# A gated FFN on Trainium2: up-projection as a 2x2 block product with seven products, down-projection as a stage of its own

## The chip, the core and the metric

The kernel runs on one core of a Trainium2 chip. TensorE (PE in the profile) multiplies, VectorE (DVE), ScalarE (ACT) and GpSimd (POOL) do the element work, and the sync engine's queue (SP) issues most transfers. The metric is the device time of one execution in microseconds (us), the median of several executions.

## The reference, cut to what matters

Two transformer blocks run one after the other on 1024 tokens of width 1024. Only the end of the second block is touched. There the reference is:

```
mix = sigmoid(ga) * (oa @ w_branch_a) + sigmoid(gb) * (ob @ w_branch_b)
x = x + mix @ w_out
h = rmsnorm(x, norm_ffn_w)
u = causal_dwconv(h @ w_up, conv_ffn_w) + conv_ffn_b      # 3 taps along the tokens
gate, up = split(u, 2, axis=-1)                           # 2816 features each
x = x + (silu(gate) * up) @ w_down
return rmsnorm(x, norm_final_w)
```

## The kernel before

All products run in fp32r with split operands. `split` takes an fp32 value to hi (an ACT cast, L59) and lo (a DVE subtraction of hi from the value, L62), and `acc3` or `gemm_fm` multiply hi by hi, hi by lo and lo by hi. So one product of a 128-row block costs three matmuls, all recorded at L41. Transposes are matmuls with the identity, recorded at L44.

The order within each engine's queue comes from a scheduler, which moves instructions of neighbouring steps past each other; each engine then runs its own queue strictly in order.

The end of the second block has these stages:

- `phase2_branch` makes the mix, feature-major, as hi and lo tiles of 8 x 128 features by 1024 tokens.
- `phase2_wout` loads x from DRAM (L1700), scales it (L1705), and adds mix @ w_out in blocks of 128 tokens by 256 columns (L1735). As the token tiles t finish, `post(t)` does the norm (ACT L1714, a chain of small DVE operations, DVE L1716), eight transposes and two splits into h hi and lo. The two halves (gate, up) of the first up-projection, `ff0`, then start.
- `phase2_ffn` runs 11 groups of two feature blocks j. For each j, gate and up are two products of 128 features by 1024 tokens, with 8 blocks of 128 inputs, 3 split products and 2 token halves: 96 matmuls of 512 columns per j, into the two-bank PSUM tiles `big`. The conv reads PSUM: an ACT identity with the first tap and the bias (L1763), and two DVE taps (L1767). Silu (ACT, L1789), the gate-up product (DVE, L1795) and its split into `ah` and `al` follow. After two j, `ah` and `al` go through the down-projection at once: 16 PSUM blocks with 6 matmuls each, and each block is added into `xs` by DVE (L1808).
- In the last group the sums of squares (L1814) and `phase2_final` (L1821 to L1831) follow each token tile: a chain of small operations, and the scaling (L1830, or ACT L1824 and POOL L1825 for t of 0 and 2), and a transfer out.

Weights come in 512 KB pieces through SP's queue, are split on ACT and DVE, and have two raw buffers (`wuraw`) and one (`wdraw`).

Of the kernel before, what the change touches and what calls it, by code (L numbers as in the profile page):

```python
# [6 lines left out]
F32 = mybir.dt.float32  # L7
F32R = mybir.dt.float32r
# [3 lines left out]
ALU = mybir.AluOpType  # L12
# [21 lines left out]
class Build:  # L34
# [1633 lines left out]
    def phase2_branch(self):  # L1668
        nc, tc, I = self.nc, self.tc, self.I
        mh = self.mp.tile([128, 8, 1024], F32R, name="mixh")  # L1670
        ml = self.mp.tile([128, 8, 1024], F32R, name="mixl")
        self.mix = (mh, ml)
        b2 = self.b2
        for sl in range(4):
            wab = self.w_b0 if sl == 0 else [
                self.load_w(b2, I[nm][sl], 256, ks=4, kb=2, tag="wa", rawbufs=2, bufs=6) for nm in ("w_ba", "w_bb")]
            for mm in range(2):
                m = sl * 2 + mm
                sg = [self.sg0[m]] if sl == 0 else []
                for a in range(len(sg), 2):  # L1680
                    t = b2.tile([128, 1024], F32, name="sg", bufs=4)
                    nc.sync.dma_start(t, self.sgd[a * 8 + m])
                    sg.append(t)
# [7 lines left out]
                self.split(mh[:, m], ml[:, m], sg[0])  # L1691

    def phase2_wout(self):
        nc, tc, I = self.nc, self.tc, self.I
        xs = self.xs = self.xp.tile([128, 8, 1024], F32, name="xs")
        hi = self.hp.tile([128, 8, 1024], F32R, name="hhi")
        lo = self.hp.tile([128, 8, 1024], F32R, name="hlo")
        self.h = (hi, lo)
        for t in range(8):
            nc.sync.dma_start(xs[:, t], self.xacc[t * 128:(t + 1) * 128, :])  # L1700
        wo = self.b2
        nf = wo.tile([128, 1024], F32, name="sg", bufs=4)
        self.load_row(nf, I["norm_final"])
        for t in range(8):
            nc.vector.scalar_tensor_tensor(xs[:, t], xs[:, t], self.r1[:, t:t + 1], nf, op0=ALU.mult, op1=ALU.mult)  # L1705

        nm = wo.tile([128, 1024], F32, name="sg", bufs=4)
        self.load_row(nm, I["norm_ffn2"])
        XN = [wo.tile([128, 1024], F32, name="sg", bufs=4) for _ in range(2)]

        def post(t):
            ss = self.sm.tile([128, 8], F32, name="ssx")[:, :1]
            xn = XN[t % 2]
            nc.scalar.activation(xn, xs[:, t], AF.Square, accum_out=ss)  # L1714
            rs = self.rsqrt(ss, 1.0 / 1024)
            nc.vector.scalar_tensor_tensor(xn, xs[:, t], rs, nm, op0=ALU.mult, op1=ALU.mult)  # L1716
            s = slice(t * 128, (t + 1) * 128)
            for f in range(0, 8, 4):
                ps = self.pa(2, 4)
                for i in range(4):  # L1720
                    self.tp(ps[:, i * 128:(i + 1) * 128], xn[:, (f + i) * 128:(f + i + 1) * 128])
                self.split(hi[:, f:f + 4, s], lo[:, f:f + 4, s], ps.rearrange("p (a b) -> p a b", a=4))
# [3 lines left out]
        for hf in range(2):  # L1726
            for n in range(4):
                W = load(I["w_out2"][n])
                for t in range(hf * 4, hf * 4 + 4):
                    ps = self.pa(0, 2)  # L1730
                    s = slice(t * 128, (t + 1) * 128)
                    for k in range(8):
                        self.acc3(ps[:, :256], (self.mix[0][:, k, s], self.mix[1][:, k, s]), W[k], k, k == 7)
                    cs = slice(n * 256, (n + 1) * 256)
                    nc.vector.tensor_add(xs[:, t, cs], xs[:, t, cs], ps[:, :256])  # L1735
# [5 lines left out]
        w = load(I["w_up2"][0])  # L1741
        self.ff0 = []
        for a in range(2):
            ps = self.big()
            self.gemm_fm(ps, w, a * 128, self.h, half_outer=True)
            self.ff0.append(ps)

    def phase2_ffn(self):
        nc, tc, I = self.nc, self.tc, self.I
        xs = self.xs  # L1750
        G = 2
        with self.pool("ff") as fp:
            nf = fp.tile([128, 1024], F32, name="nf")
            self.load_row(nf, I["norm_final2"])

            def up(j):
                return self.load_w(fp, I["w_up2"][j], 256, ks=8, kb=4, tag="wu", rawbufs=2, bufs=3)

            def conv(ps, m, parts=1):
                t = fp.tile([128, 1024], F32, name="cacc", bufs=3)  # L1760
                w = 1024 // parts
                for c in range(0, 1024, w):
                    nc.scalar.activation(t[:, c:c + w], ps[:, c:c + w], AF.Identity,  # L1763
                                         scale=self.col("conv_f", 88 + m), bias=self.col("conv_fb", m))
                    for tap in range(1, 3):
                        b = max(c, tap)
                        nc.vector.scalar_tensor_tensor(t[:, b:c + w], ps[:, b - tap:c + w - tap],  # L1767
                                                       self.col("conv_f", (2 - tap) * 44 + m), t[:, b:c + w],
                                                       op0=ALU.mult, op1=ALU.add)
                return t  # L1770

            for grp in range(11):
                A = []
                for jj in range(G):
                    j = grp * G + jj
                    if j > 1:
                        w = up(j)
                    if j:
                        acc = []
                        for a in range(2):  # L1780
                            ps = self.big()
                            end = j == 21 and a
                            self.gemm_fm(ps, w, a * 128, self.h, half_outer=end)
                            acc.append(conv(ps, j + 22 * a, 2 if end else 1))
# [219 lines left out]
```

## Time and profile before

| | us |
|---|---|
| median of 3 runs | 2929.35 (2927.75 to 2936.22) |
| the profiled execution, its own time | 2934.21 |
| its span | 2932.4 |
| PE busy | 2726.3 (93%) |
| DVE busy | 1765.5 (60%) |
| ACT busy | 1133.0 (39%) |
| POOL busy | 722.2 (25%) |

The span runs from the first to the last instruction on the chip; the execution's own time is 1.8 us longer. Shares of busy time are means over some ten stages with different limits, so the stage in question has to be read by itself: it is the last quarter of the span, from about 2150 us on. In the profile's slices POOL is at zero there up to the last 25 us.

### The profile page before, as it was taken

To read this page: it belongs to the slowest core of one execution; us is meant where nothing else is said; L and a number is where in the kernel's file an instruction comes from. 1 tells how busy PE (TensorE), PEld (TensorE's weight loads), DVE (VectorE), ACT (ScalarE), POOL (GpSimd) and SP (SyncE) were. 2 spreads that over 40 slices of the span, in tenths; PEclk is the share of its full clock that TensorE was granted. 3 is DMA by queue.
4 is the path that set the end of the run, shared out by engine and by line. 5 is a ranking of instruction groups with operands and counts; after the bars stand their busy time and mean duration, and the time that the engine had idled before them with its cause. 6 is when DMAs were issued, how large, how long until landed. Compare 5 with 4: busy or idle time off the path is not lost. (4 is left out here: it accounts for less than half of the span.)

```text
span 2932.4 us, 36530 instructions
## 1 busy us (share of the span) xinstructions
PE 2726.3 (93%) x14132; PEld 2183.9 (74%) x14132; DVE 1765.5 (60%) x2641; ACT 1133.0 (39%) x1762; POOL 722.2 (25%) x686
## 2 busy tenths in 40 slices
PE   6999998889948999699999899999999999999997
PEld 3886675555737777588889788778898888888886
DVE  3655568786687998756436333576565554455545
ACT  4445554444225666543321223463143222222223
POOL 1004425444344877412121332220000000000000
PEclk8999999999968999899999999999999999999999
DMA  6113300000567999512453544303432111111111
GB/s 223 41 57 112 106 37 1 1 22 33 172 221 255 373 373 362 171 42 88 158 182 116 185 150 141 100 23 110 164 100 67 51 57 44 50 51 43 44 36 58
DMA packets 180845, 338.75 MB, mean 116 GB/s; under 512 B 17672, under 2 KB 105736, under 8 KB 178368
## 3 DMA queue, kind: packets, MB, share of 16 engines
q1 hardware_dynamic: 162272, 270.13, 27.6%
q0 software_dynamic: 18400, 66.28, 7.1%
q8 instruction: 111, 1.82, 0.3%
q14 instruction: 62, 0.51, 0.1%
HBM read 282.88 MB, written 53.49 MB: 115 GB/s over the span
## 5 line engine op out<-in xcount | busy, mean ns | idle before, releaser
L62 DVE TENSOR_TENSOR mlo<-mraw,mhi 128x2048 fp32r<-128x2048 f32 x63 | 225.0, 3597 | 10.6 <-ACT mhi L59 10.6
L41 PE MATMUL big<-hhi,whi 128*128 128x512 f32 x656 | 210.6, 400 | 0.0
L41 PE MATMUL big<-hhi,wuhi 128*128 128x512 f32 x672 | 209.8, 389 | 0.0
L41 PE MATMUL big<-hlo,whi 128*128 128x512 f32 x656 | 208.6, 396 | 0.0
L41 PE MATMUL big<-hhi,wulo 128*128 128x512 f32 x672 | 208.2, 389 | 0.0
L41 PE MATMUL big<-hlo,wuhi 128*128 128x512 f32 x672 | 208.2, 389 | 0.0
L41 PE MATMUL big<-hhi,wlo 128*128 128x512 f32 x656 | 207.5, 395 | 0.0
L59 ACT CAST mhi<-mraw 128x2048 fp32r<-128x2048 f32 x96 | 181.7, 1912 | 55.4 <-PE big L41 29.3
L62 POOL TENSOR_TENSOR mlo<-mraw,mhi 128x2048 fp32r<-128x2048 f32 x33 | 165.5, 5022 | 74.9 <-ACT mhi L59 74.1
L1825 POOL TENSOR_TENSOR wuraw<-wuraw,nf 128x1024 f32<-128x1024 f32 x2 | 5.8, 2898 | 718.8 <-ACT rst L100 714.8
L1808 DVE TENSOR_TENSOR xs<-xs,t 128x512 f32<-128x512 f32 x176 | 117.9, 685 | 83.3 <-PE t L41 83.2
L1767 DVE SCALAR_TENSOR_TENSOR cacc<-big,cols,cacc 128x1023 f32<-128x1023 f32 (+2 forms) x90 | 113.1, 1257 | 76.6 <-ACT cacc L1763 74.9
L62 DVE TENSOR_TENSOR wlo<-wraw,whi 128x512 fp32r<-128x512 f32 (+5 forms) x124 | 80.6, 660 | 124.9 <-ACT whi L59 124.4
L41 PEld LDWEIGHTS big<-hhi,wuhi 128*128 128x128 f32 x672 | 126.2, 188 | 26.2
L41 PEld LDWEIGHTS big<-hhi,wulo 128*128 128x128 f32 x672 | 126.1, 188 | 26.2
L41 PEld LDWEIGHTS big<-hlo,wuhi 128*128 128x128 f32 x672 | 126.1, 188 | 26.2
L805 ACT ACTIVATE P<-t 128x512 f32<-128x512 f32 x160 | 95.1, 598 | 129.4 <-PE t L41 127.2
L41 PEld LDWEIGHTS big<-hlo,whi 128*128 128x128 f32 x656 | 122.9, 189 | 26.3
L41 PEld LDWEIGHTS big<-hhi,wlo 128*128 128x128 f32 x656 | 122.8, 189 | 26.0
L41 PE MATMUL t<-wdhi,ah 128*128 128x512 f32 x352 | 137.8, 391 | 1.4 <-ACT ah L59 1.2
L41 PEld LDWEIGHTS big<-hhi,whi 128*128 128x128 f32 x656 | 121.0, 189 | 23.6
L41 PE MATMUL t<-wdlo,ah 128*128 128x512 f32 x352 | 137.2, 390 | 0.0
(607 smaller groups left out, 6939.0 us busy)
## 6 DMA issues: line engine op xcount, KB each, us to landing
mraw<-in_w_gate SPq DMA_DIRECT2D x32, 1024.0 KB, 12.9
mraw<-in_w_up SPq DMA_DIRECT2D x32, 1024.0 KB, 13.3
mraw<-in_w_down SPq DMA_DIRECT2D x32, 1024.0 KB, 9.9
wmod<-in_w_mod SPq DMA_DIRECT2D x48, 512.0 KB, 5.9
wuraw<-in_w_up SPq DMA_DIRECT2D x42, 512.0 KB, 3.5
wraw<-in_w2a SPq DMA_DIRECT2D x72, 256.0 KB, 2.8
wdraw<-in_w_down SPq DMA_DIRECT2D x22, 512.0 KB, 3.2
gxd<-gx POOLq DMA_DIRECT2D x8, 1024.0 KB, 5.0
```

The lines of the kernel that those rows point to most:

```text
L41: self.nc.tensor.matmul(out, lhsT, rhs, start=start, stop=stop)
L59: nc.scalar.copy(hi, src)
L62: (nc.vector if lo_eng == "dve" else nc.gpsimd).tensor_sub(lo, src, hi.bitcast(F32))
L805: nc.scalar.activation(P, ps, AF.Exp, scale=self.sc_mla)
L1767: nc.vector.scalar_tensor_tensor(t[:, b:c + w], ps[:, b - tap:c + w - tap], self.col("conv_f", (2 - tap) * 44 + m), t[:, b:c + w], op0=ALU ...
L1808: nc.vector.tensor_add(xs[:, t, cs], xs[:, t, cs], ps)
L1825: nc.gpsimd.tensor_mul(y, y, nf)
```

## The change

**What it does.** The inputs of the up-projection (1024 features) are cut in two halves of 512, and so are the tokens. For one j the weights are four blocks (gate and up, by two feature halves) and h is four blocks (two feature halves by two token halves). Instead of eight block products, Winograd's form of Strassen's scheme takes seven, P1 to P7, each with 4 k-blocks and 3 split products: 12 matmuls of 512 columns, 84 per j. The sums that it needs are:

- of h, once: B11, B21, t1, t2 (in pool `hp3`, made in `post` and `put`) and t3, t4, B22 (made by `late` in buffers of the mix);
- of the weights, per j: S0, S1, S2, S4, four POOL operations of 128x512 on SBUF (L1834, L1835, L1852, L1857);
- of the products, per j: five DVE additions of a PSUM bank and an SBUF tile (L1844, L1851, L1855, L1861, L1865), two ACT copies out of PSUM (L1841, L1847), and two POOL additions on SBUF (L1859, L1864).

All seven weight operands per j are split after the sums (7 ACT casts, 7 DVE subtractions of 128x512). The products now land in four single-bank PSUM tiles in rotation, the sums go to four SBUF buffers for gate and up in turns, and the conv reads those (ACT L1824, DVE L1826). The gate-up product runs on POOL (L1868), and POOL's queue sends it to DRAM as `zd[j]` (L1869). x goes to DRAM too (`xsd`).

After the 22 j, the down-projection runs for each half of the tokens: 11 pairs of j, each with z reloaded and split, w_down reloaded and split, and 48 matmuls into eight PSUM banks that collect over all 22 j. So the number of its matmuls stays at 1056, and the DVE additions into `xs` fall from 176 to 16. w_down is loaded and split twice. `phase2_final` now runs for four token tiles at each half's end. The number of 128x128 transposes after w_out rises from 64 to 112.

```diff
     def phase2_wout(self):
...
+        def post(t):
+            normed(t)
+            x = XN[t]
+            if t < 4:
+                put("11", t, x[:, :512])
+                put("21", t, x[:, 512:])
+                return
+            y = XN[t - 4]
+            t2 = b3.tile([128, 512], F32, name="t2", bufs=2)
+            nc.vector.tensor_sub(y[:, :512], x[:, :512], y[:, :512])
+            nc.vector.tensor_sub(t2, x[:, 512:], y[:, :512])
+            put("t1", t - 4, y[:, :512])
+            put("t2", t - 4, t2)
+            nc.gpsimd.tensor_sub(x[:, :512], x[:, 512:], x[:, :512])
+            nc.gpsimd.tensor_sub(y[:, 512:], y[:, 512:], t2)
...
+        late("t3", "mh1", [XN[4 + i][:, :512] for i in range(4)])
+        late("t4", "ml1", [XN[i][:, 512:] for i in range(4)])
+        late("22", "mh0", [XN[4 + i][:, 512:] for i in range(4)])
...
     def phase2_ffn(self):
...
-            for grp in range(11):
...
-                        ah = fp.tile([128, 1024], F32R, name="ah", bufs=2 * G)
...
-                        nc.vector.tensor_add(xs[:, t, cs], xs[:, t, cs], ps)
...
+            for j in range(22):
+                raw = raw_of(I["w_up2"][j].rearrange("p (b n) -> p b n", b=4))
+                S = [fp.tile([128, 512], F32, name="S", bufs=3) for _ in range(3)]
+                nc.gpsimd.tensor_add(S[0], raw[:, 2], raw[:, 3])
+                nc.gpsimd.tensor_sub(S[1], S[0], raw[:, 0])
+                if j > 1:
+                    p1 = self.prod(self.pa(), op(raw[:, 0]), B["11"])
+                else:
+                    p1, p2 = self.ff0[j]
+                s = self.fa.tile([128, 512], F32, name="s", bufs=2)
+                nc.scalar.copy(s, p1)
+                p6 = self.prod(self.pa(), op(S[1]), B["t2"])
+                u2 = half(0)
+                nc.vector.tensor_add(u2, p6, s)
+                p5 = self.prod(self.pa(), op(S[0]), B["t1"])
+                c5 = half(1)
+                nc.scalar.copy(c5, p5)
+                if j > 1:
+                    p2 = self.prod(self.pa(), op(raw[:, 1]), B["21"])
+                g, u = gu(), gu()
+                nc.vector.tensor_add(g[:, :512], p2, s)
+                nc.gpsimd.tensor_sub(S[2], raw[:, 0], raw[:, 2])
+                p7 = self.prod(self.pa(), op(S[2]), B["t3"])
+                u3 = half(2)
+                nc.vector.tensor_add(u3, p7, u2)
+                S4 = fp.tile([128, 512], F32, name="S", bufs=3)
+                nc.gpsimd.tensor_sub(S4, raw[:, 1], S[1])
+                u4 = half(3)
+                nc.gpsimd.tensor_add(u4, u2, c5)
+                p3 = self.prod(self.pa(), op(S4), B["22"])
+                nc.vector.tensor_add(g[:, 512:], p3, u4)
+                tg = conv(g, j)
+                p4 = self.prod(self.pa(), op(raw[:, 3]), B["t4"])
+                nc.gpsimd.tensor_add(u[:, 512:], u3, c5)
+                nc.vector.tensor_add(u[:, :512], p4, u3)
+                tu = conv(u, j + 22)
+                nc.scalar.activation(tg, tg, AF.Silu)
+                nc.gpsimd.tensor_mul(tg, tg, tu)
+                nc.gpsimd.dma_start(self.zd[j], tg)
...
+                for bt in range(2):
...
+                    for kp in range(11):
+                        z = gu()
+                        for kk in range(2):
+                            nc.sync.dma_start(z[:, kk * 512:(kk + 1) * 512],
+                                              self.zd[kp * 2 + kk, :, bt * 512:(bt + 1) * 512])
...
-        if t in (0, 2):
+        if t in (4, 6):
```

**The loop.** DVE's queue before, over the end of one group and the next two j (`wuraw`, `wdraw` are raw weights, hi and lo their split, `cacc` the conv):

```order
L62 TENSOR_TENSOR wdlo<-wdraw,wdhi 128x1024 x2
L1767 SCALAR_TENSOR_TENSOR cacc<-big,cols,cacc 128x1023
L1767 SCALAR_TENSOR_TENSOR cacc<-big,cols,cacc 128x1022
L62 TENSOR_TENSOR wulo<-wuraw,wuhi 128x1024 x2
L1767 SCALAR_TENSOR_TENSOR cacc<-big,cols,cacc 128x1023
L1767 SCALAR_TENSOR_TENSOR cacc<-big,cols,cacc 128x1022
L1795 TENSOR_TENSOR cacc<-cacc 128x1024
L62 TENSOR_TENSOR al<-cacc,ah 128x1024
```

and DVE's queue now, in the middle of the loop, with the number of each buffer (`Ah` and `Al` are a split operand, `raw` raw weights, `ml0` the SBUF buffers of the sums, `t0` to `t3` PSUM banks, `s` the copy of P1):

```order
L62 TENSOR_TENSOR Al_19966<-raw_19957,Ah_19965 128x512
L1826 SCALAR_TENSOR_TENSOR cacc_19800<-ml0_18520,cols_73,cacc_19800 128x1023
L1826 SCALAR_TENSOR_TENSOR cacc_19800<-ml0_18520,cols_73,cacc_19800 128x1022
L62 TENSOR_TENSOR Al_19985<-S_19960,Ah_19984 128x512
L1844 TENSOR_TENSOR ml0_18520<-t1_19833,s_19831 128x512
L62 TENSOR_TENSOR Al_20003<-S_19959,Ah_20002 128x512
L62 TENSOR_TENSOR Al_20021<-raw_19957,Ah_20020 128x512
L1851 TENSOR_TENSOR ml0_18520<-t3_19869,s_19831 128x512
L62 TENSOR_TENSOR Al_20040<-S_19961,Ah_20039 128x512
L1855 TENSOR_TENSOR ml0_18520<-t0_19888,ml0_18520 128x512
```

POOL's queue before, from w_out to the end (three rows of norm weights, then the two products of `phase2_final`):

```order
L829 DMA sg_17036<-in_norm_final 128x1024
L829 DMA sg_17046<-in_norm_ffn2 128x1024
L829 DMA nf_18409<-in_norm_final2 128x1024
L1825 TENSOR_TENSOR wuraw_22459<-wuraw_22459,nf_18409 128x1024
L1825 TENSOR_TENSOR wuraw_22526<-wuraw_22526,nf_18409 128x1024
```

and POOL's queue now, one j of the loop, eight rows that come 22 times:

```order
L1835 TENSOR_TENSOR S_19960<-S_19959,raw_19957 128x512
L1864 TENSOR_TENSOR ml0_18520<-ml0_18520 128x512
L1852 TENSOR_TENSOR S_19961<-raw_19957 128x512
L1868 TENSOR_TENSOR cacc_19777<-cacc_19777,cacc_19800 128x1024
L1869 DMA zd_18516<-cacc_19777 128x1024
L1857 TENSOR_TENSOR S_20056<-raw_19957,S_19960 128x512
L1834 TENSOR_TENSOR S_20109<-raw_20107 128x512
L1859 TENSOR_TENSOR ml0_18520<-ml0_18520 128x512
```

The taps moved from PSUM to SBUF operands, the additions into `xs` and the gate-up product left DVE, the splits of weight sums stand between the additions of the j before, and POOL has work in the loop.

**The start of the FFN.** PE's queue before, at the last transposes (`sg` is the normed tile, `big` the first up-projection):

```order
L44 MATMUL t_18216<-ident,sg 128x128 x4
L44 MATMUL t_18223<-ident,sg 128x128 x4
L41 MATMUL big<-hhi,walo 128x512
L41 MATMUL big<-hhi,wahi 128x512
L41 MATMUL big<-hlo,wahi 128x512
L41 MATMUL big<-hhi,walo 128x512
```

and now (t3 and t4 are put out of buffers of `mh` and `ml`, `B21` is an operand of P2, `Bt2` of P6):

```order
L41 MATMUL big<-B21l,wahi 128x512
L41 MATMUL big<-B21h,walo 128x512
L44 MATMUL t_18427<-ident,ml_17603 128x128 x4
L44 MATMUL t_18434<-ident,ml_17603 128x128 x4
L44 MATMUL t_18441<-ident,ml_17603 128x128 x4
L44 MATMUL t_18448<-ident,ml_17603 128x128 x4
L44 MATMUL t_18456<-ident,mh_17602 128x128 x4
L44 MATMUL t_18463<-ident,mh_17602 128x128 x4
L44 MATMUL t_18470<-ident,mh_17602 128x128 x4
L44 MATMUL t_18477<-ident,mh_17602 128x128 x4
L41 MATMUL t_18534<-Bt2h,Ah 128x512
L41 MATMUL t_18534<-Bt2l,Ah 128x512
```

Eight groups of four transposes now stand in a row, with no product between them, ahead of the loop's first matmul.

**From up to down.** SP's queue now, at the end of the loop, with the engines and queues that a row waits for in brackets (before, w_down's loads stand between those of w_up, and nothing is reloaded):

```order
L1809 DMA raw_21779<-in_w_down2 128x2x1024 [waits DMAHW3_49,DVE_49,Pool_49]
L1809 DMA raw_21855<-in_w_down2 128x2x1024 [waits DMAHW4_49,DVE_49,Pool_49]
L1881 DMA xt_21769<-xsd_17069 128x1024 [waits DMASW0_49,PE_49]
L1881 DMA xt_21771<-xsd_17069 128x1024 [waits DMASW1_49]
L1881 DMA xt_21773<-xsd_17069 128x1024
L1881 DMA xt_21775<-xsd_17069 128x1024
L1881 DMA xt_22699<-xsd_17069 128x1024
L1881 DMA xt_22701<-xsd_17069 128x1024
L1881 DMA xt_22703<-xsd_17069 128x1024 [waits DMAHW5_49]
L1885 DMA ml0_18520<-zd_18516 128x512 [waits DMASW0_49,DMAHW6_49,DVE_49,Activation_49]
L1885 DMA ml0_18520<-zd_18516 128x512 [waits DMAHW7_49,DMASW1_49]
L1881 DMA xt_22705<-xsd_17069 128x1024 [waits DMAHW0_49,DMASW7_49]
```

Seven of the eight loads of x stand ahead of the first z. That z goes into a buffer of gate and up, which DVE and ACT must have read for the last time; the raw weights of the down-projection are ahead of it in the queue.

## Rows read from the trace of the kernel before

**Rows 1.** Windows: stretch, length, busy us (count) by engine, PE clock, DMA share, GB/s
```profile
2485.00:2550.00 65.00, 65.00 (x287) 53.54 (x286) 32.79 (x34) 14.89 (x14) 0.00 (x0) 1.00 0.16 49
2875.00:2932.40 57.40, 41.00 (x179) 32.98 (x177) 38.26 (x89) 21.11 (x50) 5.80 (x2) 0.90 0.19 74
```

**Rows 2.** Timeline of PE in the FFN: start, us, instruction, count
```profile
2503.38 0.62 PE L41 MATMUL big<-hhi,wuhi 128*128 128x512 f32 x2
2503.83 0.62 PE L41 MATMUL big<-hlo,wuhi 128*128 128x512 f32 x2
```

**Rows 3.** Timeline of PE at transposes and gaps (idle before, releaser in brackets)
```profile
2097.56 0.39 PE L41 MATMUL t<-wahi,mixh 128*128 128x256 f32 x1 [2.21 <-DVE xs L1735]
...
2098.48 0.42 PE L41 MATMUL t<-wahi,mixh 128*128 128x256 f32 x1
2098.70 0.41 PE L41 MATMUL t<-walo,mixh 128*128 128x256 f32 x1
...
2101.67 0.28 PE L41 MATMUL t<-wahi,mixh 128*128 128x256 f32 x1
2101.79 0.28 PE L41 MATMUL t<-walo,mixh 128*128 128x256 f32 x1
...
2186.51 1.06 PE L44 MATMUL t<-ident,sg 128*128 128x128 f32 x8 [1.47 <-DVE sg L1716]
2187.33 0.37 PE L41 MATMUL t<-wahi,mixl 128*128 128x256 f32 x1
...
2897.52 0.50 PE L41 MATMUL t<-wdhi,ah 128*128 128x512 f32 x1 [1.15 <-ACT ah L59]
```

**Rows 4.** Groups by form, 2000 to 2933 us: count, busy us, mean ns, idle
```profile
L1808 DVE TENSOR_TENSOR xs<-xs,t 128x512 f32<-128x512 f32 x176 | 117.9, 685 | 83.3 <-PE t L41 83.2
...
L62 DVE TENSOR_TENSOR walo<-waraw,wahi 128x512 fp32r<-128x512 f32 x48 | 32.9, 688 | 23.5 <-ACT wahi L59 23.2
L59 ACT CAST wahi<-waraw 128x512 fp32r<-128x512 f32 x48 | 29.8, 621 | 105.2 <-PE t L41 37.2 <-PE big L41 28.7 <-DMA waraw<-in_w_out 21.3
...
L1716 DVE SCALAR_TENSOR_TENSOR sg<-xs,rsy,sg 128x1024 f32<-128x1024 f32 x8 | 10.3, 1285 | 0.2
L1705 DVE SCALAR_TENSOR_TENSOR xs<-xs,r,sg 128x1024 f32<-128x1024 f32 x8 | 10.0, 1276 | 0.3 <-DMA xs<-xacc 0.3
```

**Rows 5.** POOL: one line's durations (ns min/median/max), then two groups by form
```profile
L812 POOL TENSOR_TENSOR acc<-acc,P x64: 1259/1277/2588, 455.8 to 723.7; 128x512 f32<-128x512 f32 x64
...
L1122 POOL TENSOR_TENSOR xn<-x,nf 128x1024 f32<-128x1024 f32 x6 | 14.3, 2379 | 19.1 <-DMA x<-xacc 11.8 <-PE t L44 7.2
...
L1295 POOL DMA_DIRECT2D sgd<-sg x16 | 9.0, 565 | 84.1 <-ACT sg L1294 84.1
```

**Rows 6.** One tile's durations on DVE, then timelines of POOL and DVE
```profile
L62 DVE TENSOR_TENSOR mlo<-mraw,mhi x63: 2274/2291/7146, 898.7 to 1198.2; 128x2048 fp32r<-128x2048 f32 x63
...
1012.68 4.61 POOL L62 TENSOR_TENSOR mlo<-mraw,mhi 128x2048 fp32r<-128x2048 f32 x1 [2.78 <-ACT mhi L59]
...
1012.77 1.21 DVE L62 TENSOR_TENSOR xl<-big,xh 128x1024 fp32r<-128x1024 f32 x1
...
1015.09 4.35 DVE L62 TENSOR_TENSOR mlo<-mraw,mhi 128x2048 fp32r<-128x2048 f32 x1
...
1050.70 6.35 POOL L62 TENSOR_TENSOR mlo<-mraw,mhi 128x2048 fp32r<-128x2048 f32 x1 [2.81 <-ACT mhi L59]
...
1050.28 2.28 DVE L62 TENSOR_TENSOR mlo<-mraw,mhi 128x2048 fp32r<-128x2048 f32 x1
```

**Rows 7.** Transfers of the last 50 us: KB each, median us to landing
```profile
out<-cacc SPq DMA_DIRECT2D x8, 256.0 KB, 2.0
```

**Rows 8.** The end: PE's last matmul (timeline), then pieces of the chain
```profile
2917.01 0.39 PE L41 MATMUL t<-wdhi,al 128*128 128x512 f32 x1
...
2926.49 0.17 DVE rst L103
...
2926.88 0.75 DVE cacc L1830
```

More of the change, by code (lines that the diff above doesn't have):

```diff
@@ L1669, in phase2_branch @@
         nc, tc, I = self.nc, self.tc, self.I
-        mh = self.mp.tile([128, 8, 1024], F32R, name="mixh")
-        ml = self.mp.tile([128, 8, 1024], F32R, name="mixl")
-        self.mix = (mh, ml)
+        self.mix = [[self.mp.tile([128, 8, 512], F32R, name=f"m{w}{hf}") for w in "hl"] for hf in range(2)]
         b2 = self.b2
@@ L1708, in phase2_wout @@
+        nm = b3.tile([128, 1024], F32, name="row")
         self.load_row(nm, I["norm_ffn2"])
-        XN = [wo.tile([128, 1024], F32, name="sg", bufs=4) for _ in range(2)]
-        def post(t):
[L1712 to L1722, printed above, removed]
+        XN = []
@@ L1724, in load, with early @@
+        def early(j, b):
+            raw = wo.tile([128, 512], F32, name="waraw", bufs=2)
+            nc.sync.dma_start(raw, I["w_up2"][j, :, b * 512:(b + 1) * 512])
+            A = [wo.tile([128, 512], F32R, name=f"wa{w}", bufs=6) for w in ("hi", "lo")]
+            self.split(*A, raw)
+            return A
         def load(src):
@@ L1740, in phase2_wout @@
                     post(2 * n + 1)
[L1741 to L1746, printed above, removed]
+            if hf == 0:
+                for w in "hl":
+                    v = self.mp.tile([128, 4, 1024], F32, name=f"m{w}0")
+                    XN += [v[:, i] for i in range(4)]
+        E = {(j, b): early(j, b) for b in range(2) for j in range(2)}
@@ new lines, in phase2_wout, with late @@
+        ab = [self.big() for _ in range(2)]
+        self.ff0 = [[self.prod(ab[j][:, b * 512:(b + 1) * 512], E[j, b], B[nm]) for b, nm in enumerate(("11", "21"))]
+                    for j in range(2)]
+        def late(op, slot, srcs):
+            v = self.mp.tile([128, 8, 512], F32R, name=slot)
+            B[op] = v[:, :4], v[:, 4:]
+            for i, src in enumerate(srcs):
+                put(op, i, src)
+        late("t3", "mh1", [XN[4 + i][:, :512] for i in range(4)])
+        late("t4", "ml1", [XN[i][:, 512:] for i in range(4)])
@@ new lines, in op, with conv @@
+            def op(src):
+                A = [fp.tile([128, 512], F32R, name=f"A{w}", bufs=8) for w in "hl"]
+                self.split(*A, src)
+                return A
+            fp.tile([128, 1024], F32, name="cacc", bufs=3)
+            for w in "hl":
+                fp.tile([128, 512], F32R, name=f"A{w}", bufs=8)
+            fp.tile([128, 512], F32, name="S", bufs=3)
+            def conv(x, m):
+                t = fp.tile([128, 1024], F32, name="cacc", bufs=3)
+                nc.scalar.activation(t, x, AF.Identity, scale=self.col("conv_f", 88 + m), bias=self.col("conv_fb", m))
+                for tap in range(1, 3):
+                    nc.vector.scalar_tensor_tensor(t[:, tap:], x[:, :1024 - tap],
+                                                   self.col("conv_f", (2 - tap) * 44 + m), t[:, tap:],
+                                                   op0=ALU.mult, op1=ALU.add)
+                return t
```

178 lines of the change are left out of this document (97 added, 81 removed).

## The prediction, made before the changed kernel was run

> **What bounds the kernel now.** I read the table of windows first. In the FFN's stretches, of which one row stands for nine alike, PE is busy for all of 65.00 us with 287 matmuls at full clock, DVE for 32.8, ACT for 14.9 and POOL for nothing [rows 1]. That is 0.2265 us per matmul of 512 columns, and the timeline of PE shows the same: two matmuls start 0.45 us after the two before them [rows 2]. No gap is left, so a matmul taken out is worth its 0.2265 us for as long as nothing else takes PE's place. The last stretch differs: PE has its last matmul at 2917.01, some 0.4 us long, and the span ends at 2932.4 [rows 1, 8]; the 15 us behind it belong to DVE's norm and scaling of the last token tiles and to the last transfer. In w_out, ahead of the FFN, PE waits at times for the norm: 1.47 us ahead of one pair of transposes [rows 3].
>
> The sum is made against the profiled execution's own 2934.2 us; the median of the runs is 4.9 us below it, and I take that off at the end.
>
> **The change part by part.**
>
> *Products.* 22 j with 84 matmuls instead of 96: 264 fewer, by 0.2265 us: **-59.8 us**. The down-projection keeps its 1056.
>
> *Transposes.* 48 more of 128x128. Eight take 0.82 us from the first's start to the next matmul [rows 3], 0.10 each: **+4.9**.
>
> *Start of the FFN.* For each of the last four token tiles DVE now has the addition and the small operations of the norm (about 1 us), the scaling (1.29), two subtractions and two splits (four by 0.69) [rows 4]: about 5 us, so 20 for four, 3 more for the four splits of the first weights, and 5.5 for the eight splits behind the late transposes: 28.5 us. PE has in the same stretch 72 matmuls of w_out at 0.12 us (8.6; the spacing is in rows 3), the 48 matmuls of `ff0` (10.9), which need only the first four tiles and so fill in, and 64 transposes (6.4): 26 us. So DVE is late by 2.5 us, and the chain from the last tile's product to its first transposes (norm, scaling, subtraction) and POOL's two subtractions of 1.28 for t3 and B22 stand partly bare: another 4. Against this goes the 1.47 us wait of before; but a wait of 2.21 us was followed by matmuls 0.22 us apart instead of 0.12, from 2098 to 2101.7 [rows 3], half clock, which costs 1.8. Together **+6.5**, between 3 (DVE's excess alone) and 12 (the whole chain bare, clock lost twice).
>
> *The loop.* PE needs 84 x 0.2265 = 19.03 us per j. No other engine needs as much by itself: DVE 7 splits of 0.69, 4 taps of 1.28 and 5 additions of 0.685 (13.3) [rows 4]; POOL 6 sums of 1.28, a product of 2.38 and 0.57 for the issue (10.6) [rows 5]; ACT 7 casts of 0.62 and the copies, identities and silu, about 9. But the trace shows DVE and POOL in each other's way. DVE's 2048-column subtraction takes 2.29 us at the median; the one that began at 1015.09 beside POOL's (1012.68, 4.61 us long, to 1017.29) took 4.35, to 1019.44, which is 2.15 behind POOL's end: it waited for POOL and then ran. The other way round, POOL's of 1050.70 took 6.35 us and ended 4.49 behind DVE's end at 1052.56, where 4.61 is normal. The subtraction with a PSUM operand at 1012.77 was not held up, at 1.21 us [rows 6]. So a DVE instruction on two SBUF operands and a POOL instruction exclude each other, less some 0.13 us at each change. Before, the taps and most of DVE's work in the loop read PSUM or had no POOL work beside them. Now the splits (4.8), the taps (5.1) and POOL's operations (7.7 + 2.4) all belong to the excluding kind: 20.0 us per j, and about 19.4 if four to five changes per j save 0.13 each. Only the 3.4 us of additions from PSUM run beside POOL.
>
> The Trainium skill ("SBUF — State Buffer", section "Who interferes with whom") says this as a rule: a DVE instruction with two SBUF inputs contends with a GpSimd instruction that reads SBUF, the pair of ports is held for a whole instruction, and one with at most one SBUF input does not contend. It speaks against this change, which moves operands from PSUM to SBUF and puts POOL beside them; the trace agrees with it (4.35 us against 2.29). Without it the loop would cost nothing above PE, and the sum would be 9 us lower.
>
> Over the loop that makes 20 x 19.4 + 2 x 18 = 424 us for the pair (the first two j lack two splits each) and 20 x 19.03 + 2 x 13.6 = 408 for PE (the first two j have 60 matmuls each, since P1 and P2 come from `ff0`). Of the 16 us, the sums and splits for the first j lie ahead of the loop (about 4), and the last taps fall into the next term (about 3): **+9**. It is 0 where each exclusion falls into time that PE's four rotating banks cover, and 30 where the order of the queues adds 1 us per j to the pair.
>
> *From up to down.* The first z is loaded into a buffer that the last j's conv must have left. From the end of the last product: addition 0.69, second tap 1.28 [rows 4], the load of 256 KB 2.0 (the out transfers of that size [rows 7]), casts of z and of w_down, 0.62 each, and issue and semaphores, about 1.5 by estimate from these rows: 6.7 us without a matmul; before there was no such gap. After it comes half clock as above, 1.8: **+8.5**, between 6 (the load at once) and 13 (the load behind those of x, of 512 KB each, which stand ahead of it on SP). The reload of w_down and the second split cost nothing while PE takes 10.9 us per 48 matmuls and DVE 4.1: PE covers them.
>
> *Between the token halves.* All eight banks are held; the second half starts as its first banks are read out: 0 to 2, **+1**.
>
> *The end.* The 1.15 us wait for the last `ah` [rows 3] goes: **-1.2**. Behind the last matmul stand now four token tiles' work instead of eight's: addition 0.69, square 0.62, the chain of seven small operations (about 0.15 each [rows 8]), two scalings 1.4, and from the start of the last scaling's second half at 2927.6 to the span's end 4.8, together 8.6; with 1.6 of backlog of the tile before it 10.2 instead of 15.0: **-4.8**, between -6 and -3.
>
> Sum: -59.8 + 4.9 + 6.5 + 9 + 8.5 + 1 - 1.2 - 4.8 = **-35.9**, so 2898.3 on the profiled execution's scale, **2893** on the median's.
>
> **The rivals.**
>
> 1. *The exclusion hides.* Each wait falls into the time that the four banks cover, and PE stays the bound: loop 0, start 5, transition 7: -59.8 + 4.9 + 5 + 7 + 0.5 - 1.2 - 5 = -48.6, time 2881. For it: DVE's 13.3 and POOL's 10.6 leave each engine room, and PSUM additions run beside POOL. Against it: the pair's 19.4 to 20.0 are above PE's 19.03.
>
> 2. *The pair is the bound, and the order adds to it.* DVE's queue is strict: splits for the next j stand between additions that wait for PE, and POOL's 2.38 us product can hold up a split that PE wants next. With 20.5 us per j the loop term is 29.4 + 9 - 11 = 27: time 2911. For it: DVE's queue in the order of the changed kernel has a split ahead of nearly every addition. Against it: a late split hurts only if no other product is ready, and eight operand buffers (four products) run ahead.
>
> 3. *Slower.* The additions from PSUM don't find POOL work beside them, so DVE and POOL simply alternate: 20.0 + 3.4 = 23.4 us per j, loop term 87 - 2 = 85, time 2969; waits over 2 us per j at half clock would add to it. It decides from about 21.4 us per j, where the loop eats the other terms' 45 us; from 21.8 the time is slower by over 0.3%. For it: in-order queues on both sides, with POOL's two additions waiting for DVE's and DVE's for POOL's in the same j (u4 behind u2, g's second half behind u4). Against it: DVE and POOL take up work in turns in the trace, with 0.13 us saved rather than lost at each change.
>
> That the change does not do what it says is excluded: PE's queue has the 264 matmuls less.
>
> **How the numbers follow.** My forecast (2886 to 2904) has 0.38, rival 1 (below 2886) 0.20, rival 2 (2904 to 2921) 0.20. Between rival 2 and 3, from 2921 to 2938, lie 0.09, and above that 0.13. About 0.3% is what a measurement of this kernel can tell from no change, 2920.6 to 2938.1: faster 0.78, same 0.09, slower 0.13. The bounds of the unknown terms taken together give 2874 (start 3, loop 0, transition 6, end -6) and 2923 (start 12, loop 30, transition 13); to leave no more than 2 in 10 out, the range goes up to 2932: 2874 to 2932.
>
> **What would show it.** The table of windows: PE busy nearly all of each stretch of the loop and 19.0 to 19.6 us from j to j; 20.5 or more, with waits of PE's weight loads for DVE's splits, would be rival 2 or 3. The durations of splits and taps in the loop: many at their alone time plus a POOL instruction's (a 0.69 split at 2 us) show the exclusion. A gap of 6 to 7 us between the last product of the loop and the first of the down-projection, with half clock behind it. 10 us from the last matmul to the end. The forecast is wrong if waits of over 2 us recur in each j, since the clock then halves too.

## The result, and the profile after

The changed kernel takes 2907.51 us (median of 4, 2904.12 to 2910.93), the kernel before in the same comparison 2931.89. The ratio is 0.9917, with a 95% interval of 0.9896 to 0.9937: faster by 24 us, clear of the 0.3% that can be told from no change. The forecast was 2893, the range 2874 to 2932.

The profiled execution took 2910.93 us, its span is 2909.1. The page's first lines, and windows of the second half (columns as in [rows 1]):

```profile
span 2909.1 us, 37112 instructions
PE 2678.8 (92%) x13916; PEld 2145.0 (74%) x13916; DVE 1872.5 (64%) x2789; ACT 1236.1 (42%) x2020; POOL 1010.3 (35%) x878
```

```profile
2089.00:2155.00 66.00, 56.35 (x447) 55.79 (x446) 33.41 (x58) 17.26 (x30) 3.26 (x6) 0.92 0.53 178
...
2210.00:2220.00 10.00, 6.79 (x28) 5.08 (x28) 9.76 (x14) 2.05 (x4) 3.81 (x3) 0.83 0.30 107
...
2450.00:2500.00 50.00, 50.00 (x222) 41.40 (x221) 42.84 (x44) 23.74 (x33) 30.19 (x21) 1.00 0.23 84
...
2650.00:2700.00 50.00, 46.11 (x191) 37.60 (x192) 18.80 (x30) 16.14 (x30) 2.93 (x2) 0.91 0.52 178
...
2850.00:2909.00 59.00, 46.84 (x206) 38.09 (x204) 26.35 (x55) 18.81 (x41) 4.75 (x2) 0.94 0.24 85
```

The loop (2450 to 2500) is to be set against the FFN's row in [rows 1]: PE has no gap and full clock in both, though DVE and POOL are far busier. What was lost lies around the loop. The timeline of PE lists its waits there (before, 2.21, 1.47 and 1.15 us [rows 3]):

```profile
2105.05 0.58 PE L41 MATMUL t<-wahi,mh 128*128 128x256 f32 x1 [9.57 <-DVE xs L1767]
...
2197.17 0.63 PE L44 MATMUL t<-ident,mh 128*128 128x128 f32 x4 [2.21 <-DVE mh L1740]
...
2211.83 0.87 PE L44 MATMUL t<-ident,mh 128*128 128x128 f32 x4 [1.94 <-DVE rsy L101]
...
2238.14 0.97 PE L41 MATMUL t<-mh,Ah 128*128 128x512 f32 x3 [3.88 <-ACT mh L59]
...
2653.88 0.80 PE L41 MATMUL big<-Ah 128*128 128x512 f32 x1 [8.52 <-ACT Ah L59]
...
2896.45 0.39 PE L41 MATMUL t<-Ah,Al 128*128 128x512 f32 x1
```

Six more waits of 0.24 to 1.11 us, 4.4 us together, stand between the first and the fourth row. All waits of PE from w_out on sum to 30.5 us, against 5.1 before (the three named and one of 0.25).

The first wait was 2.21 us before. Timelines of POOL, SP and DVE there:

```profile
2095.14 0.57 POOL L829 DMA_DIRECT2D row<-in_norm_final  x1 [146.75 <-PE t L41]
...
2092.62 4.01 SPq L1706 DMA_DIRECT2D xs<-xacc  x8
...
2103.19 1.28 DVE L1711 SCALAR_TENSOR_TENSOR xs<-xs,r,row 128x1024 f32<-128x1024 f32 x1 [8.62 <-DMA row<-in_norm_final]
```

DVE scales x with the norm row (L1711) before it can read w_out's first PSUM tiles. The row's transfer starts at 2095.1, 2.5 us after the first of the eight loads of x (4 MB), and lands at 2103.2. The trace names PE as what POOL waited for, but PE had long been done. The program's waits show the real one: the row's buffer lies in the changed kernel over the tile that the last mix split (DVE, ended 2094.6) reads. Before, the row was issued 7.0 us ahead of the first load of x. Timelines of POOL and SP before:

```profile
2081.41 0.57 POOL L829 DMA_DIRECT2D sg<-in_norm_final  x1 [134.06 <-ACT wahi L59]
...
2088.41 4.37 SPq L1700 DMA_DIRECT2D xs<-xacc  x8
```

### The profile page after: what moved, and what is told of

The parts are those of the page before. It is cut to its first block, busy times and chain, and to the rows that moved or that the text cites. A ratio compares the mean times of both kernels' runs of the same rounds, so it can differ in the third digit from the quotient of the medians.

```text
span 2909.1 us, 37112 instructions
## 1 busy us (share of the span) xinstructions
PE 2678.8 (92%) x13916; PEld 2145.0 (74%) x13916; DVE 1872.5 (64%) x2789; ACT 1236.1 (42%) x2020; POOL 1010.3 (35%) x878
## 4 chain that ended last, share of the span: by engine, by line
PE 49%; DVE 4%; issue 1%; DMA 1%; ACT 1%; POOL 0%; SPq 0%; DVEq 0%; ACTq 0%; POOLq 0%
PE t L41 25%; PE big L41 22%; PE t L44 2%; DVE Rb L1396 1%; DVE bP L1593 0%; DVE Rt L1395 0%; DMA waraw<-in_w_out 0%; DVE xs L1711 0%; DMA row<-in_norm_final 0%; DVE mm L1589 0%; ACT bPT L1611 0%; DVE ml L1721 0%; DVE walo L62 0%; DMA ml<-zd 0%; DMA waraw<-in_w_up 0%
## 5 line engine op out<-in xcount | busy, mean ns | idle before, releaser
L62 DVE TENSOR_TENSOR Al<-raw,Ah 128x512 fp32r<-128x512 f32 x150 | 117.4, 784 | 134.9 <-ACT Ah L59 134.9
L59 ACT CAST Ah<-raw 128x512 fp32r<-128x512 f32 x150 | 92.7, 620 | 213.6 <-PE t L41 209.7
L1826 DVE SCALAR_TENSOR_TENSOR cacc<-ml,cols,cacc 128x1023 f32<-128x1023 f32 x88 | 123.8, 1407 | 9.0 <-ACT cacc L1824 8.3
L812 POOL TENSOR_TENSOR acc<-acc,P 128x512 f32<-128x512 f32 x64 | 86.9, 1358 | 115.4 <-ACT P L805 115.0
L62 DVE TENSOR_TENSOR Al<-S,Ah 128x512 fp32r<-128x512 f32 x88 | 120.0, 1366 | 3.6 <-ACT Ah L59 3.6
L700 DVE TENSOR_REDUCE mm<-big 128x1 f32<-128x640 f32 x128 | 101.3, 816 | 23.9 <-PE big L41 22.8
L41 PE MATMUL t<-mh,Ah 128*128 128x512 f32 x352 | 108.5, 389 | 3.9 <-ACT mh L59 3.9
L41 PE MATMUL t<-whi,hlo 128*128 128x344 f32 (+2 forms) x320 | 108.3, 338 | 2.7 <-DVE hlo L62 1.5
L41 PE MATMUL t<-whi,hhi 128*128 128x344 f32 (+2 forms) x320 | 109.4, 342 | 0.7 <-DVE hhi L61 0.3
L41 PE MATMUL t<-mlo,xh 128*128 128x512 f32 x256 | 101.9, 398 | 7.7 <-POOL mlo L62 4.7
```

The lines of the kernel that those rows point to most:

```text
L41: self.nc.tensor.matmul(out, lhsT, rhs, start=start, stop=stop)
L59: nc.scalar.copy(hi, src)
L62: (nc.vector if lo_eng == "dve" else nc.gpsimd).tensor_sub(lo, src, hi.bitcast(F32))
L700: nc.vector.reduce_max(r[:, a * 2 + 1 - e:a * 2 + 2 - e], ps.rearrange("p (a b) -> p a b", a=2)[:, :, :320], axis=AX.XY)
L812: eng.tensor_add(u["acc"][e], u["acc"][e], P)
L1826: nc.vector.scalar_tensor_tensor(t[:, tap:], x[:, :1024 - tap], self.col("conv_f", (2 - tap) * 44 + m), t[:, tap:], op0=ALU.mult, op1=ALU.add)
```

## The experiments

All are made from the changed kernel, and each gives its ratio to the kernel before (interval in brackets). A ratio 0.001 above or below 0.9917 is 2.9 us; the difference of two such ratios is known to 5 to 9 us. What is given as a trace's time runs from w_out's first product to the end of the span, since what lies ahead of it, untouched by these edits, differs by up to 10 us from trace to trace. It is 819.7 us in the changed kernel and 843.5 before.

**e1: the norm row early.**

```diff
+        b3.tile([128, 512], F32, name="t2", bufs=2)
+        b3.tile([128, 1024], F32, name="pad")
         nf = b3.tile([128, 1024], F32, name="row")
         self.load_row(nf, I["norm_final"])
```

> The changed kernel with one thing moved: the norm row that w_out's residual is scaled with gets a buffer that is free one mix tile earlier (it lay over the last tile that the mix is split from, whose last reader is DVE at 2094.6 us). Theory A (the 9.57 us gap of PE at 2105 comes from the row's transfer, which was issued at 2095.1 behind eight loads of x that had the DMA engines at 400 GB/s): the row lands before the loads of x, the gap falls to about the 2.2 us of the kernel before, total -7 to -8 us against the changed kernel's 2907.5, so about 2900. Theory B (the gap comes from the loads of x themselves, the row only being the last to be seen): the gap stays above 7 us, total within 2 us of 2907.5.

Ratio 0.9873 (0.9855 to 0.9891), 2897.40 us. PE's wait there, in the timeline:

```profile
2099.51 0.39 PE L41 MATMUL t<-wahi,mh 128*128 128x256 f32 x1 [2.69 <-DVE xs L1769]
```

9.57 became 2.69 us: theory A, and the loads of x themselves are no cause. The trace's time falls by 7.2 us, as much as the wait; the ratio's change, 13 us with some 8 us of uncertainty, is not in conflict with it.

**e2: z in buffers of its own.**

```diff
+                dn.tile([128, 1024], F32, name="zt", bufs=2)
                 nf = dn.tile([128, 1024], F32, name="nf")
...
-                        z = gu()
+                        z = dn.tile([128, 1024], F32, name="zt", bufs=2)
```

> The changed kernel with z reloaded, in the down-projection, into two buffers of its own, which lie over the operands of P1 (read for the last time some 16 us before the loop's last product), instead of the buffers of gate and up of the last j. Theory A (the 8.52 us gap between up and down is the wait for that buffer, the load behind it and the casts): the load is done in time, a gap of 2 to 3 us stays, since the first cast of w_down stands on ACT behind the conv's last identity; the half clock behind the gap shrinks or goes; total -6 to -9 us, about 2900. Theory B (the gap is set by ACT and DVE, which have the last conv and six splits to do before the first products): the gap stays at 6 us or more, total -0 to -2.

Ratio 0.9895 (0.9877 to 0.9914), 2902.14 us. PE's first matmul of the down-projection, and ACT ahead of it:

```profile
2644.84 1.22 PE L41 MATMUL big<-Ah 128*128 128x512 f32 x2 [4.45 <-ACT Ah L59]
...
2642.52 0.62 ACT L59 CAST Ah<-zt 128x512 fp32r<-128x512 f32 x1 [2.76 <-DMA zt<-zd]
2643.05 1.24 ACT L1824 ACTIVATE cacc<-ml,cols 128x1024 f32<-128x1024 f32 x1
2644.19 0.60 ACT L59 CAST Ah<-raw 128x512 fp32r<-128x512 f32 x1
```

The gap fell from 8.52 to 4.45, between the two theories (the trace's time by 4.5): half was the buffer. Of the rest, 2.1 us go by until z has landed (PE's last product ends at 2640.4, z's cast starts at 2642.52); z's load still stands behind four loads of x. The other 2.3 are ACT's order, where the last conv's identity stands ahead of w_down's cast.

**e3: no sums of weights.** The four POOL lines (L1834, L1835, L1852, L1857) are out.

```diff
-                nc.gpsimd.tensor_add(S[0], raw[:, 2], raw[:, 3])
-                nc.gpsimd.tensor_sub(S[1], S[0], raw[:, 0])
...
-                p6 = self.prod(self.pa(), op(S[1]), B["t2"])
+                p6 = self.prod(self.pa(), op(raw[:, 2]), B["t2"])
```

> The changed kernel without POOL's four sums of weights per j (raw weight blocks are split in their place, so the products are of other weights; all else stays, 7 splits, 4 taps, 5 additions on DVE and two additions and the product on POOL). The excluding work of DVE and POOL falls from about 20 to about 14.9 us per j. The prediction's term for the loop (+9 us of waiting that DVE and POOL cause there): total about -9, 2898. Rival (PE's queue has no gap in the loop, so the exclusion is hidden there): only the 3.9 us gap and POOL's part in the loop's first j can change, total 0 to -4; splits of weights and taps take 0.69 and 1.28 us nearly always.

Ratio 0.9889 (0.9873 to 0.9905), 2900.95 us. In the loop behind its first products nothing changed, since PE had no gap there to lose. The gain is at the loop's start: the 3.88 us wait is 0.67, and PE's waits from the late transposes on sum to 4.1 instead of 6.6 us; from w_out's first wait to the loop's end the trace is 5.9 us shorter. So the rival holds for the loop. The total (8 us by the ratios with as much uncertainty, 6.5 by the trace) is past its 0 to -4, since the start gave more than it had allowed.

**e4, e11, e12: POOL's last sum three, two and five times.**

```diff
                 nc.gpsimd.tensor_sub(S4, raw[:, 1], S[1])
+                nc.gpsimd.tensor_sub(S4, raw[:, 1], S[1])
+                nc.gpsimd.tensor_sub(S4, raw[:, 1], S[1])
```

> The changed kernel with POOL's last sum of weights made three times over in each j: 2.56 us more of excluding POOL work per j. By the prediction's account (DVE and POOL take turns at 19.4 to 20.0 us per j against PE's 19.03) the pair needs 22 us, 3 us above PE: total +55 to +60 us, about 2965, and gaps in PE in each j. If the pair has slack (it needs 18 us or less, the overlap at each change being larger than taken or much of POOL's time falling beside additions from PSUM): 20.5 us or less, total +0 to +30. If POOL's time is not additive at all to DVE's (no exclusion): 0.

> The changed kernel with POOL's last sum of weights made twice per j, 1.28 us more. With two extra the loop ran at 20.55 us per j. If each extra adds its whole 1.28 us to what DVE and POOL need together, that need is 18.0 us without an extra, and one extra gives 19.3 us, 0.2 to 0.3 above PE's 19.03: about +5 us against the changed kernel, 2912, with small gaps in PE in some j. If the two extras met a step (a chain that only they lengthen): 19.03 us per j and no gaps, 2906 to 2909.

> The changed kernel with POOL's last sum of weights made five times per j, 5.1 us more. If the need adds up (18.0 + 5.1): 23.1 us per j, total about +90, 2997. If DVE and POOL overlap more when POOL has more to do: 22 us or less, below 2975. If in-order waits come on top: 24 us or more.

Ratios: two more 1.0041 (1.0026 to 1.0056), one more 0.9938 (0.9917 to 0.9960); four more, 2997.43 us in one run. The loop's pace is read from ACT's copy of P1, once per j. Two rows in succession, of the changed kernel, then with one, two and four more:

```profile
2439.94 0.57 ACT L1841 COPY s<-t 128x512 f32<-128x512 f32 x1
2458.88 0.57 ACT L1841 COPY s<-t 128x512 f32<-128x512 f32 x1
```
```profile
2446.28 0.57 ACT L1841 COPY s<-t 128x512 f32<-128x512 f32 x1
2465.36 0.57 ACT L1841 COPY s<-t 128x512 f32<-128x512 f32 x1
```
```profile
2439.01 0.57 ACT L1841 COPY s<-t 128x512 f32<-128x512 f32 x1
2459.56 0.57 ACT L1841 COPY s<-t 128x512 f32<-128x512 f32 x1
```
```profile
2492.15 0.57 ACT L1841 COPY s<-t 128x512 f32<-128x512 f32 x1
2515.41 0.57 ACT L1841 COPY s<-t 128x512 f32<-128x512 f32 x1
```

These rows are 18.9, 19.1, 20.6 and 23.3 us apart; over nine late j the means are 19.02, 19.06, 20.55 and 23.25. From two to four more, each costs 1.35 us: beyond PE's 19.03 something with POOL's operations in it is the bound, and they add up there. A straight line back from these two runs gives 17.9 us per j for the changed kernel, and 19.2 with one more. That is an estimate, and a little high: with one more the loop ran at 19.06 with gaps in its first seven j alone, which was the second of that run's expectations (19.03 and no gaps), not the first (19.3 with small gaps). The expectation of 22 us for two more was too high.

What makes up the pace beyond PE's was not shown apart. DVE's wait in the run with four more:

```profile
2506.99 1.22 DVE L62 TENSOR_TENSOR Al<-S,Ah 128x512 fp32r<-128x512 f32 x1 [6.47 <-ACT Ah L59]
```

In each j of the middle of the loop DVE is idle there for 6.47 us, and for 3.73 with two more, until ACT has cast the sum that POOL makes behind the added ones. So the pace may come from DVE and POOL in each other's way, or from the order of POOL's queue alone. Both would grow by about one POOL operation for each added sum (1.28 us long, 1.37 from the start of one to that of the next).

**e5: PE's order at the loop's start by hand.** P6 and P5 of the first j get the late transposes for t4 and B22 between their k-blocks; PE's order is fixed for the first two j.

```diff
+            for _ in self.late[0]:
+                pass
...
-                p6 = self.prod(self.pa(), op(S[1]), B["t2"])
+                p6 = self.prod(pa(0), op(S[1]), B["t2"], L[0])
...
+                    p5 = self.prod(pa(1), op(S[0]), B["t1"], L[1])
```

> The changed kernel with PE's order at the start of the loop set by hand: four groups of late transposes (t3), then P6 of the first j with the four for t4 between its k-blocks, P5 with the four for B22, then P7, P3, P4; before, all twelve stood around P6, and three matmuls of P7 and P3 stood ahead of P5. Theory A (the gaps from 2222 to 2238 us, 1.11 + 0.81 + 0.80 + 3.88, and the half clock behind them come from this order, evacuation by evacuation): most of the 6.6 us and 1 to 2 us of clock go, total -5 to -9 us, about 2900. Theory B (DVE and POOL are behind there with subtractions, sums and splits, and PE would wait for them in any order): the gaps move to P6's or P5's operands, total -0 to -3.

Ratio 0.9908 (0.9890 to 0.9926), 2907.55 us. PE's waits from the late transposes on (a fourth, of 1.10, ahead of these):

```profile
2226.55 0.51 PE L41 MATMUL t<-Bt2h,Ah 128*128 128x512 f32 x1 [1.19 <-ACT Ah L59]
...
2233.86 1.12 PE L44 MATMUL t<-ident,mh 128*128 128x128 f32 x4 [2.36 <-DVE ml L62]
...
2243.43 0.70 PE L41 MATMUL t<-mh,Ah 128*128 128x512 f32 x2 [1.56 <-DVE mh L62]
```

6.2 us where it was 6.6, and the trace's time is 0.4 us shorter: theory B. P6 started earlier, but its operands and the transposes' splits then had to be waited for. DVE and ACT are behind there in this order too.

**e6: POOL's late subtractions on DVE.**

```diff
-            nc.gpsimd.tensor_sub(x[:, :512], x[:, 512:], x[:, :512])
-            nc.gpsimd.tensor_sub(y[:, 512:], y[:, 512:], t2)
+            nc.vector.tensor_sub(x[:, :512], x[:, 512:], x[:, :512])
+            nc.vector.tensor_sub(y[:, 512:], y[:, 512:], t2)
```

> The changed kernel with the two subtractions per token tile that POOL makes for t3, t4 and B22 moved to DVE (0.6 us each there, 1.28 on POOL), for the last four token tiles. In the changed kernel's trace DVE's small operations of the norm (two inputs in SBUF, 0.15 us) took 1.1 to 1.3 us beside these subtractions. Theory A (the exclusion on the norm's chain causes the 2.21 + 1.94 + 0.51 + 0.94 us gaps of PE there): no small operation above 0.5 us, the four gaps fall by 2 to 4 us, total -2 to -5. Theory B (DVE's own work bounds this stretch): DVE gets 4.8 us more, the gaps stay or grow by up to 3, total 0 to +4.

Ratio 0.9903 (0.9886 to 0.9921), 2905.61 us: not to be told from the changed kernel. The waits for the norm fell from 5.8 to 5.0 us, less than theory A's 2 to 4; those behind it changed places, and one small operation still takes 1.23 us, beside a sum of weights on POOL. The trace's time is 3.1 us shorter, but that of e7, whose edit touches only the end, is 2.5 us shorter ahead of the loop, so this shows nothing either. The exclusion on the norm's small operations is plainly there (below); by these traces it is worth some 3 us at most of the 12.4 us of waits in this stretch.

**e7: one tile fewer through POOL at the end.**

```diff
-        if t in (4, 6):
+        if t == 4:
```

> The changed kernel with only token tile 4, not 4 and 6, scaled by ACT and POOL at the end. In the changed kernel a DVE operation of 0.16 us in the last tile's norm took 2.11 us beside POOL's product at 2901.6. Theory A (the exclusion lengthens the end): the time from PE's last matmul to the span's end falls from 12.4 to 10 to 11 us. Theory B (DVE is full at the end, so that a tile more on it costs what the wait cost): 12 to 13 us.

One run, 2904.95 us. PE's last matmul starts at 2892.26 and the span ends at 2903.2: 10.9 us, where the changed kernel has 2909.1 - 2896.45 = 12.7. Theory A, -1.7.

**e10: an eighth product, as work only.**

```diff
+                A3 = op(raw[:, 3])
+                self.prod(self.pa(), A3, B["t4"])
-                p4 = self.prod(self.pa(), op(raw[:, 3]), B["t4"])
+                p4 = self.prod(self.pa(), A3, B["t4"])
```

> The changed kernel with an eighth block product per j put back as work only: P4's 12 matmuls are done twice, the first time into a bank that nobody reads; sums, splits, additions, taps and stages stay. If PE bounds the loop (22 x 12 x 0.2265): +59.8 us against the changed kernel, about 2967, that is 36 us above the kernel before, which is then the price of all else in the change. If DVE and POOL bound it in part, or the first j catch up behind PE: less than +55.

Ratio 1.0100 (1.0085 to 1.0116), 2962.51 us: 54 us above the changed kernel by the ratios, with some 7 us of uncertainty. In the trace the loop, from its first product to its last, takes 475.1 instead of 415.5 us: 59.6 more, as expected of a loop that PE bounds. Part of that comes back behind the loop, where the gap to the down-projection is 5.36 instead of 8.52 us:

```profile
2703.69 1.22 PE L41 MATMUL big<-Ah 128*128 128x512 f32 x2 [5.36 <-ACT Ah L59]
```

So seven products for eight are worth 59.6 us in the loop, some 54 in all, and everything that was built around them costs 29 us against the kernel before.

**e8 and e9: three gaps closed.** e8 has the edits of e1, e2 and e7, and loads x and the last norm row only at the fourth pair of the down-projection; e9 has that of e6 too.

```diff
                     for kp in range(11):
-                        z = gu()
+                        if bt == 0 and kp == 3:
+                            self.load_row(nf, I["norm_final2"])
+                        for i in range(4 if kp == 3 else 0):
+                            t = bt * 4 + i
+                            xt[t] = dn.tile([128, 1024], F32, name="xt", bufs=8)
+                            nc.sync.dma_start(xt[t], self.xsd[t * 128:(t + 1) * 128, :])
```

> Three moves together on the changed kernel: the norm row's early buffer, z's own buffers with the reloads of x pushed behind the first loads of z (so that the first casts of z and w_down stand on ACT ahead of the last conv), and only token tile 4 through ACT and POOL at the end. Theory (the three gaps add): 7 us at the row, 8.5 us and 2 us of half clock between up and down, 1.7 us at the end: about -19 against 2907.5, so 2888, ratio to the kernel before 0.985; no gap above 1 us between the last product of the loop and the down-projection. Rival (a gap closed at one place opens at another, since DVE has the last conv and the splits to do either way): the gap moves into the first 48 matmuls of the down-projection, total only -9 to -12.

> The three moves, and POOL's subtractions for the late operands on DVE. If the exclusion on DVE's norm chain costs time at the start of the FFN: 2 to 3 us less than with the three moves alone. If the chain's own length bounds it: within 1 us.

e8: ratio 0.9838 (0.9825 to 0.9852), 2884.39 us; e9: 0.9839 (0.9826 to 0.9853), 2885.56. In e8 the casts of the first z and w_down stand ahead of the last conv on ACT. The window around the change of stages, and the first matmuls of the down-projection, with no wait:

```profile
2600.00:2650.00 50.00, 50.00 (x223) 41.39 (x222) 36.07 (x40) 20.34 (x32) 17.44 (x12) 1.00 0.53 186
```
```profile
2634.11 0.39 PE L41 MATMUL big<-Ah 128*128 128x512 f32 x1
2634.34 0.39 PE L41 MATMUL big<-Al,Ah 128*128 128x512 f32 x1
```

The gains add: -23 us by the ratios and -19.9 by the traces, where -19 was expected, and no wait opened elsewhere. e9 is not to be told from e8 by its time, which could hide the 2 to 3 us in question; its trace is 0.8 us shorter than e8's. That leans to the chain's own length (theory B of e6) and does not settle it. Both beat the kernel before by 1.6%.

## Why the prediction was right, and where its steps were not

The direction, the range and the main term were right; the loss outside that term was put at 24 us and is 36.5 by the same subtraction (59.8 - 23.3, on the profiled executions). The forecast's own band (2886 to 2904) missed the 2907.5, which lies in the band of rival 2 (2904 to 2921), though rival 2's loop is not there. That the sum came so near is in part luck: 9 us for the loop that were not lost stand against a wait that was not seen and a start and a transition that were sized too small. (The lower of the prediction's two bounds adds up to 2876, not 2874; nothing hangs on it.)

| step | forecast | in the trace |
|---|---|---|
| 264 products less | -59.8 | -59.8 by the count at 0.2265 us; 59.6 in e10's loop |
| 48 transposes more | +4.9 | not apart from the start |
| wait for the norm row | not seen | +7.4 (9.57 instead of 2.21) |
| start of the FFN | +6.5 | +11.0 of waits, about +7 of half clock and small losses |
| the loop | +9 | 0 |
| from up to down | +8.5 (6.7 of wait, 1.8 of half clock) | 8.52 of wait, 2.9 of half clock |
| between the halves | +1 | 0.2 |
| wait at the end | -1.2 | -1.4 |
| tail | -4.8 | -2.7 |

The column's sum with the 4.9 is -22.0, against -23.3 measured; the 1.3 us are not placed.

**The step that was missing** is the norm row. The prediction took w_out's beginning as unchanged. The diff moves the row from one pool's buffers (`b2`, next to the weights) to the first place of a new pool, and where that lies decides when the load may start. Issued behind eight loads instead of ahead of them, it kept DVE idle for 8.62 us; e1, which issues it ahead of them again (2085.5, the first load at 2093.95), takes the wait away.

**The start was sized too small.** DVE is the loaded engine there, as forecast (busy 9.76 of the 10 us from 2210 to 2220, some 3 of them spent waiting for POOL), but the term let `ff0` fill in for the whole of it. The nine waits there read as chains instead: scaling, subtraction, transposes, cast, split, one tile behind the other, and PE's two banks for transposes. One item had no place in the sum at all: POOL's subtractions hold up DVE's smallest operations. Timelines of POOL and DVE:

```profile
2205.48 1.62 POOL L1744 TENSOR_TENSOR ml<-ml 128x512 f32<-128x512 f32 x1
2207.07 1.29 POOL L1745 TENSOR_TENSOR mh<-mh,t 128x512 f32<-128x512 f32 x1
...
2205.87 1.25 DVE L102 SCALAR_TENSOR_TENSOR rst<-rsy 128x1 f32<-128x1 f32 x1
...
2207.15 1.22 DVE L103 TENSOR_TENSOR rst<-rst,rsv 128x1 f32<-128x1 f32 x1
```

Each of these DVE operations takes 0.16 us alone. With those subtractions moved to DVE (e6, e9) most of the waits stayed, so this is at most a small part. What of the rest is chain and what DVE's load is open: e5 only showed that PE's order is not it.

**The loop was rival 1's.** The exclusion is real: groups of the loop, 2250 to 2630 us (columns as in [rows 4]):

```profile
L62 DVE TENSOR_TENSOR Al<-S,Ah 128x512 fp32r<-128x512 f32 x80 | 113.5, 1419 | 0.0
...
L1852 POOL TENSOR_TENSOR S<-raw 128x512 f32<-128x512 f32 x20 | 36.1, 1807 | 0.0
...
L1861 DVE TENSOR_TENSOR ml<-t,ml 128x512 f32<-128x512 f32 x21 | 14.5, 690 | 18.0 <-PE t L41 9.6 <-POOL ml L1859 7.1 <-POOL S L1835 1.2
```

A split of a weight sum, 0.69 us alone [rows 4], takes 1.42 on the mean of the loop, with POOL at work beside it, an addition with a PSUM operand 0.69 as ever. That is the rule that the prediction took from the Trainium skill ("SBUF — State Buffer", "Who interferes with whom"), and the trace agrees on which operations exclude each other. It does not agree on the sum: by a pair of ports held for whole instructions the two would need 20.0 us per j and 21.3 with one more sum; e11 ran at 19.06. The step that failed is the pair's need of 19.4, the sum of the durations less 0.13 us at each of four to five changes between the engines. By the line through e4 and e12 the need is some 17.9 us, 2.1 below the sum of durations, which would be sixteen such changes; that it is these changes was not shown apart. What was shown is the distance to the edge: one more sum on POOL fits under PE's pace, two do not. The prediction's last sign, that waits of over 2 us in each j would halve the clock, did not hold either: in e12 PE waits 2.1 to 2.2 us in most j, at a granted clock of 0.95 to 1.00.

**From up to down** had the right chain and was sized too small: 6.7 us of wait and 1.8 of half clock were forecast, together 8.5. The wait alone is 8.52, and it is chance that the two figures agree. The load of z, put at 2.0 us, took 4.7 to the cast that waited for it. Timelines of SP and ACT:

```profile
2647.90 0.80 SPq L1885 DMA_DIRECT2D ml<-zd  x2
...
2652.68 0.62 ACT L59 CAST Ah<-ml 128x512 fp32r<-128x512 f32 x1 [3.71 <-DMA ml<-zd]
```

Half of the wait is the buffer (e2), half the order on ACT and z's place behind the loads of x (e2 against e8). Half clock behind it cost 2.9 us instead of the 1.8 taken from [rows 3]. Timeline of PE, 0.42 us apart, then 0.24:

```profile
2656.56 0.63 PE L41 MATMUL big<-Ah,Al 128*128 128x512 f32 x1
2656.98 0.63 PE L41 MATMUL big<-Ah 128*128 128x512 f32 x1
...
2659.40 0.40 PE L41 MATMUL t<-Ah 128*128 128x512 f32 x1
2659.64 0.40 PE L41 MATMUL t<-Al,Ah 128*128 128x512 f32 x1
```

**The tail** lost 2 us to the same exclusion, in the last tile's norm (e7 gives 1.7 of them back):

```profile
2901.63 2.34 POOL L1921 TENSOR_TENSOR y<-y,nf 128x1024 f32<-128x1024 f32 x1 [5.44 <-ACT y L1920]
...
2901.88 2.11 DVE L102 SCALAR_TENSOR_TENSOR rst<-rsy 128x1 f32<-128x1 f32 x1
```

## What to carry to other kernels

Where a change trades TensorE work for element work on two other engines, as here, the steady loop can be the smaller risk: compare its period with what the pair needs together, and look for the losses at the loop's two ends, where a stage begins with a load into a buffer that the stage before has only just left. Such a wait cost the load's place in the queue on top of the buffer's delay, and other places for a few tiles and loads took it away (e1, e8). Put no GpSimd work on SBUF beside a chain of small VectorE operations that ends the program (e7).

## What was not expected of the hardware

DVE operations on a single column with two SBUF operands were held up until a POOL instruction beside them had ended: 0.16 us became 1.25 and 2.11. Together DVE and POOL needed some 2.1 us per j less than the sum of their excluding durations (17.9, by estimate from e4 and e12, against 20.0). From two added POOL operations to four, each of 1.28 us cost 1.35.
